# Ending the weight sums of a decoder trunk's down projection inside the gate/up groups, with a new table of rank shifts

## The chip, the cores and the metric

The kernel runs on one core of a Trainium2 chip. TensorE (PE, with its weight loads as PEld), VectorE (DVE), ScalarE (ACT), GpSimd (POOL) and SyncE (SP) each work through a queue of their own, in a fixed order, and meet at semaphores. The metric is the device time of one execution in microseconds (us): 2087.72 us as the median of 3 runs before the change (2087.07 to 2088.88).

## The reference

The reference is a decoder trunk of two layers over 1024 tokens of width 1024, in float32:

```python
for l in range(DEPTH):
    h = rmsnorm(x, attn_norm[l])
    proj = h @ w_in[l]                      # split into ten parts for four token mixers
    ...                                     # latent attention, gated convolution, pooling, window attention
    x = x + mixed @ w_o[l]
    h2 = rmsnorm(x, ffn_norm[l])
    gate, up = jnp.split(h2 @ w_gate_up[l], 2, axis=-1)
    x = x + (jax.nn.silu(gate) * up) @ w_down[l]
return rmsnorm(x, final_norm)
```

The feed-forward width is 2816. The change lies in the last two products, `w_gate_up` and `w_down`.

## The kernel before, in words

**Products.** Activations are held transposed, features on the 128 partitions, in two halves of 512 tokens. Each float32 operand is split into a high and a low part of type float32r: ACT casts the high part (L281) and DVE subtracts it for the low part (L282). Three matmuls of 128x512 (high-high, high-low, low-high, L270) then stand for one float32 product.

**Gate and up.** Both feed-forward products use a seven-product scheme on 2x2 blocks in place of eight products. The gate/up stage has 22 groups `f`; groups 1 to 21 go through one loop. A group forms seven sums of 12 matmuls, partly on top of one another in the same PSUM bank. Where a partial sum is needed twice, ACT copies it out of the bank (`snap`, L1180), and the next 12 matmuls on this bank wait for that copy. A group has three such copies: after the first sum, after the second sum on the same bank, and after the first sum on the other bank (`ps_mm`). The results of two groups are combined on DVE (`combos`) and written to HBM buffers `ad1` to `ad6` (L1329), and one half goes to `ad0` (L1461).

**Down.** The down stage has 28 units: seven products times four row blocks, 33 matmuls each. Each unit loads its weights (L1375), from `w_dn` or from the buffer `qd`, and its activations (L1392, L1395) from `ad`, and splits both on ACT and DVE.

**The sums of down weights.** `qd` holds four sums of blocks of `w_down`, as the scheme needs them. The generator `dn_sums` makes them in 22 pieces: load 512 KB (L155), four DVE adds (L159), store 512 KB to `qd` (L162). It yields three times a piece, so 66 steps lead to the last add, and a 67th issues the last store. Each loop group takes three steps (`next(sums, None)`), the last group none: 60 steps. The first five down units take three steps each, which is where the other pieces end.

**Buffers.** SBUF is 47 slots of 128x1024 float32, handed out by the program in its written order (`u17_7140` is the tile with number 7140, in slot 17). A load into a slot waits on SP until the last user of that slot is done. If that user is a store, SP waits until the store has landed, with all that is queued behind it.

**The order.** The order of the queues is not the order of the code. A planner (`order_engines`, `arrange`) takes all instructions with an estimated duration and a rank, which is the place in the program plus a shift, and lets each engine take the ready instruction with the lowest rank. The shifts stand in the table `MOVED`, as pairs of group and shift. The order that comes out is fixed for each engine: if on the chip an instruction is late, all behind it on that engine wait.

All loads and stores named here go through SP's queue.

Of the kernel before, what the change touches and what calls it, by code (L numbers as in the profile page):

```python
# [111 lines left out]
def trunk_kernel(ctx: ExitStack, tc: tile.TileContext, ins, out):  # L112
# [266 lines left out]
    for l in range(L):  # L379
# [84 lines left out]
        for t in range(2):  # L464
            f = tmp()
# [988 lines left out]
        for f in range(NPL, NFF):  # L1454
# [37 lines left out]
            if not end:  # L1492
                next(sums, None)
# [804 lines left out]
```

## Time and profile before

| What | Value |
|---|---|
| Median of 3 runs | 2087.72 us |
| Profiled execution, its own time | 2087.91 us |
| Its span, first to last instruction | 2086.1 us |
| PE busy | 2046.0 us, 98% of the span |
| DVE busy / ACT busy | 77% / 47% |
| Mean granted TensorE clock | 0.997 |
| Gate/up groups of the two layers | about 368 to 795 us and 1460 to 1822 us |
| Down stage, first units, of the two layers | from about 795 us and 1822 us |

The profiled execution took 1.8 us more than its span. PE counts as busy from a matmul's start to its modelled end, and matmuls overlap, so idle time of PE between matmuls is read from the rows of PE in order of time: a number in brackets at the end of a row is how long PE stood idle before it, and on what it waited. The chain of waits follows the work that ended last, back from the last instruction.

### The profile page before, as it was taken

What the parts mean: (1) busy time and instruction counts of PE and PEld (TensorE: products, weight loads), DVE (VectorE), ACT (ScalarE), POOL (GpSimd) and SP (SyncE); (2) the same over time, 40 slices, a digit from 0 to 9 for tenths busy, and PEclk for the clock granted to TensorE, in tenths of its full rate; (3) what the DMA queues carried; (4) which work ended last, traced back from release to release, by engine and by line L of the source; (5) the groups of instructions that cost most, each with busy time, mean ns of one, the idle gap of its engine ahead of it and who ended that gap; (6) DMA issues with size and microseconds to landing.
All of it is one profiled execution on the core that took longest, in us unless ns stands there. A gap on an engine that the chain in (4) does not pass through costs nothing.

```text
span 2086.1 us, 26084 instructions
## 1 busy us (share of the span) xinstructions
PE 2046.0 (98%) x9394; PEld 1666.1 (80%) x9394; DVE 1600.1 (77%) x2859; ACT 983.9 (47%) x1726; POOL 7.0 (0%) x37
## 2 busy tenths in 40 slices
PE   8999999999999999999999999999999999999997
PEld 6887887778878887788888877877878878877787
DVE  7789987997867877655656898989878787785465
ACT  6447666753333334444532576757333333354342
POOL 0000000000000000000000000000000000000000
PEclk9999999999999999999999999999999999999999
DMA  4110222345435438766411103142554444397562
GB/s 169 43 62 21 83 82 99 111 162 182 162 131 179 161 125 276 265 214 207 137 46 44 46 19 98 59 151 77 182 177 144 159 172 141 121 345 243 170 212 82
DMA packets 148817, 289.74 MB, mean 139 GB/s; under 512 B 12608, under 2 KB 72000, under 8 KB 148688
## 3 DMA queue, kind: packets, MB, share of 16 engines
q1 hardware_dynamic: 148656, 288.03, 40.7%
q8 instruction: 74, 1.21, 0.2%
q14 instruction: 55, 0.45, 0.1%
q0 software_dynamic: 32, 0.04, 0.0%
HBM read 204.66 MB, written 83.36 MB: 138 GB/s over the span
## 4 chain that ended last, share of the span: by engine, by line
PE 82%; DVE 8%; DMA 6%; ACT 2%; issue 2%; SPq 0%; DVEq 0%; ACTq 0%
PE ps_mm L270 33%; PE ps_s L270 23%; PE ps_t L270 9%; PE ps_pv L270 7%; PE ps_pv L966 2%; DVE u L282 2%; PE ps_t L954 1%; DMA u<-ad 1%; DMA u<-in_w_dn 1%; DMA ad<-u 1%; PE ps_t L328 1%; DVE u L285 1%; ACT u L281 1%; PE ps_s L900 1%; PE ps_s L901 1%
## 5 line engine op out<-in xcount | busy, mean ns | idle before, releaser
L270 PE MATMUL ps_mm<-u,u 128*128 128x512 f32 (+1 forms) x3376 | 880.8, 392 | 13.7 <-ACT u L284 7.0
L270 PEld LDWEIGHTS ps_mm<-u,u 128*128 128x128 f32 x3376 | 620.7, 189 | 149.0 <-issue 8.6
L270 PE MATMUL ps_s<-u,u 128*128 128x512 f32 x2666 | 685.1, 392 | 11.1 <-ACT tn L1180 7.1
L270 PEld LDWEIGHTS ps_s<-u,u 128*128 128x128 f32 x2666 | 497.0, 188 | 127.3 <-ACT tn L1180 13.9
L281 ACT CAST u<-u 128x1024 fp32r<-128x1024 f32 (+2 forms) x376 | 329.7, 897 | 492.2 <-PE ps_mm L270 111.5
L282 DVE TENSOR_TENSOR u<-u,u 128x1024 fp32r<-128x1024 f32 (+2 forms) x376 | 380.0, 1031 | 147.6 <-ACT u L281 122.3
L270 PE MATMUL ps_t<-u,u 128*128 128x512 f32 (+1 forms) x1122 | 294.0, 379 | 0.0
L270 PEld LDWEIGHTS ps_t<-u,u 128*128 128x128 f32 x1122 | 205.3, 188 | 41.4 <-ACT u L281 1.2
L270 PE MATMUL ps_pv<-u,u 128*128 128x512 f32 x744 | 203.3, 392 | 3.4 <-ACT u L281 1.7
L270 PEld LDWEIGHTS ps_pv<-u,u 128*128 128x128 f32 x744 | 138.3, 188 | 36.5 <-ACT u L281 3.3
L1314 ACT ACTIVATE tp<-tp 128x512 f32<-128x512 f32 x88 | 55.5, 632 | 98.3 <-DVE tp L340 98.2
L281 ACT CAST u<-ps_t 128x512 fp32r<-128x512 f32 (+3 forms) x128 | 60.1, 501 | 58.9 <-PE ps_t L954 33.2
L284 ACT ACTIVATE u<-u,par 128x512 fp32r<-128x512 f32 x100 | 69.4, 717 | 33.2 <-DVE u L1103 12.3
L282 DVE TENSOR_TENSOR u<-ps_t,u 128x512 fp32r<-128x512 f32 (+3 forms) x128 | 71.1, 576 | 13.1 <-ACT u L281 12.6
L1180 ACT COPY tn<-ps_s 128x512 f32<-128x512 f32 x64 | 37.3, 583 | 87.1 <-PE ps_s L270 87.0
L159 DVE TENSOR_TENSOR u<-u 128x256 f32<-128x256 f32 x176 | 73.9, 421 | 4.6 <-DMA u<-in_w_dn 3.0
L285 DVE SCALAR_TENSOR_TENSOR u<-u,par,u 128x512 fp32r<-128x512 f32 x100 | 72.6, 747 | 3.3 <-ACT u L284 3.2
L316 ACT ACTIVATE tn<-u 128x512 f32<-128x512 f32 (+1 forms) x93 | 52.3, 590 | 44.6 <-DVE u L1565 36.3
L214 DVE TENSOR_TENSOR u<-u,u 128x1024 fp32r<-128x1024 f32 (+1 forms) x46 | 51.8, 1128 | 25.8 <-ACT u L213 17.5
L1315 DVE TENSOR_TENSOR tp<-tp,u 128x512 f32<-128x512 f32 x88 | 60.3, 687 | 14.6 <-ACT tp L1314 14.4
L1512 DVE TENSOR_TENSOR tp<-ps_mm,tn 128x512 f32<-128x512 f32 x42 | 28.9, 689 | 49.7 <-PE ps_mm L270 49.5
L213 ACT CAST u<-u 128x1024 fp32r<-128x1024 f32 (+1 forms) x46 | 44.7, 975 | 29.7 <-DMA u<-in_w_in 11.8
(189 smaller groups left out, 2054.7 us busy)
## 6 DMA issues: line engine op xcount, KB each, us to landing
u<-in_w_gu SPq DMA_DIRECT2D x88, 512.0 KB, 4.0
ad<-u SPq DMA_DIRECT2D x154, 256.0 KB, 2.1
u<-ad SPq DMA_DIRECT2D x70, 512.0 KB, 5.1
u<-in_w_dn SPq DMA_DIRECT2D x68, 512.0 KB, 3.9
qd<-u SPq DMA_DIRECT2D x44, 512.0 KB, 3.2
u<-qd SPq DMA_DIRECT2D x32, 512.0 KB, 4.5
u<-in_w_in SPq DMA_DIRECT2D x30, 512.0 KB, 3.5
u<-in_xT SPq DMA_DIRECT2D x32, 256.0 KB, 4.5
```

The lines of the kernel that those rows point to most:

```text
L159: dve.tensor_tensor(out=o, in0=o, in1=u, op=ALU.add)
L213: act.copy(hi[:, :n], raw[:, :n])
L214: dve.tensor_tensor(out=lo[:, :n], in0=raw[:, :n], in1=rd(hi[:, :n]), op=ALU.subtract)
L270: pe.matmul(o, w, r, start=start and k == 0 and i == 0, stop=stop and k == n - 1 and i == 2, skip_group_check=again,)
L281: act.copy(hi, f)
L282: dve.tensor_tensor(out=lo, in0=f, in1=rd(hi), op=ALU.subtract)
L284: act.activation(hi, f, AF.Copy, scale=gain)
L285: dve.scalar_tensor_tensor(out=lo, in0=f, scalar=gain, in1=rd(hi), op0=ALU.mult, op1=ALU.subtract)
L316: act.activation(q, f, AF.Square)
L966: pe.matmul(py[:, c0:], v_of(j, h), R.ap(s)[:, c0:], start=j == 0 and n == 0, stop=j == nj - 1 and n == 1,)
L1314: last_silu = act.activation(g, g, AF.Silu)
L1315: dve.tensor_tensor(out=g, in0=g, in1=r, op=ALU.mult)
```

## The change

It has two parts. In the loop over the gate/up groups, the second of the three places that step `dn_sums` now takes one step in an even group and two in an odd one. Groups 1 to 20 then take 70 steps, which is over the 67 that all sums need, so that the calls in the down stage find nothing left. And the whole table `MOVED` is replaced: 1427 pairs in place of 1985, fitted with scattered DMA times.

```diff
             silu(gate, r2[0])
-            if not end:
+            for _ in range(0 if end else 1 + (f % 2)):
                 next(sums, None)
             onto(w.pa, blocks(w.sq, 0), hb[T3])
...
 MOVED = """
-1:-5.5 5:1 6:-403.5 7:-85.5 8:-2 10:5.5 11:9 12:-294.5 13:128 16:-110 17:21 19:24 20:4 22:23.5 23:45.5
...
+1:-15 5:-2.5 10:70.5 13:-497.5 16:67.5 20:-3.5 23:-3 26:-9 29:-220.5 54:-1 56:-98.5 80:-31 81:-340 82:5 83:-6
...
```

No matmul, cast, copy or DMA is added or removed. All engines' queues are put in another order. Three places show how.

**SP, where layer 0 goes from the gate/up groups to the down stage**, behind the stores to `ad` of groups 18 and 19. Before:

```order
L1375 DMA u17_7140<-in_w_dn 128x1024
L1392 DMA u31_7144<-ad0_87 128x1024
L1375 DMA u45_7141<-in_w_dn 128x384 x2
L1392 DMA u41_7165<-ad0_87 128x1024
L1392 DMA u1_7198<-ad0_87 128x1024
L162 DMA qd_94<-u15_7010 128x4x256
L155 DMA u31_7277<-in_w_dn 128x4x256
L1375 DMA u15_7463<-in_w_dn 128x1024
L1392 DMA u41_7330<-ad1_88 128x1024
L1392 DMA u46_7146<-ad0_87 128x1024
```

And now:

```order
L1329 DMA ad6_93<-u28_7020 128x512
L1375 DMA u41_7155<-in_w_dn 128x1024
L1375 DMA u36_7156<-in_w_dn 128x384
L1392 DMA u17_7159<-ad0_87 128x1024
L1375 DMA u36_7156<-in_w_dn 128x384
L1392 DMA u45_7182<-ad0_87 128x1024
L1375 DMA u12_7177<-in_w_dn 128x1024
L1392 DMA u39_7180<-ad0_87 128x1024
L1588 DMA u17_7294<-xr_86 128x512
L1392 DMA u33_7213<-ad0_87 128x1024
```

The store of a sums piece (L162) and the load of the next (L155) no longer stand among the first loads of the down stage. Before, the load into slot 15 (`u15_7463`) came two rows behind the store that reads the same slot (`u15_7010`); now no load there follows a sums store.

**ACT and PE in the same stretch**, in the last group (f = 21). On ACT, from the first copy out of the bank `ps_s` to the second. Before:

```order
L1180 COPY tn_7119<-ps_s_7105 128x512
L281 CAST u2_7201<-u41_7165 128x1024
L281 CAST u0_2157<-u28_6826 128x512
L281 CAST u5_7179<-u46_7146 128x1024
L281 CAST u7_7169<-u17_7140 128x1024
L1314 ACTIVATE tp_7087<-tp_7087 128x512
L281 CAST u0_2157<-u45_7141 128x384
L1180 COPY tn_7160<-ps_s_7105 128x512
```

And now:

```order
L1180 COPY tn_7134<-ps_s_7120 128x512
L281 CAST u1_7216<-u39_7180 128x1024
L281 CAST u6_7220<-u45_7182 128x1024
L281 CAST u23_7296<-u12_7177 128x1024
L281 CAST u0_2157<-u36_7156 128x384
L281 CAST u10_7285<-u33_7213 128x1024
L1180 COPY tn_7175<-ps_s_7120 128x512
```

On PE, from the end of the sum that the second copy takes to the next sum on its bank. Before:

```order
L270 MATMUL ps_s_7105<-u24_4207,u40_7032 128x512
L270 MATMUL ps_mm_7183<-u22_4053,u14_7068 128x512 x2
L270 MATMUL ps_mm_7183<-u22_4053,u12_7069 128x512
L270 MATMUL ps_mm_7183<-u42_4090,u14_7068 128x512
L270 MATMUL ps_s_7105<-u8_4057,u14_7068 128x512 x2
```

And now:

```order
L270 MATMUL ps_s_7120<-u24_4207,u32_7051 128x512
L270 MATMUL ps_mm_7198<-u22_4053,u46_7085 128x512 x2
L270 MATMUL ps_mm_7198<-u22_4053,u28_7086 128x512
L270 MATMUL ps_mm_7198<-u42_4090,u46_7085 128x512 x2
L270 MATMUL ps_mm_7198<-u42_4090,u28_7086 128x512
L270 MATMUL ps_mm_7198<-u26_4172,u46_7085 128x512 x2
L270 MATMUL ps_mm_7198<-u26_4172,u28_7086 128x512
L270 MATMUL ps_mm_7198<-u34_4210,u46_7085 128x512 x2
L270 MATMUL ps_mm_7198<-u34_4210,u28_7086 128x512
L270 MATMUL ps_s_7120<-u8_4057,u46_7085 128x512 x2
```

On ACT five casts of freshly loaded down tiles now stand between the two copies, where four stood (with one cast of a gate/up weight and one SiLU). On PE 12 matmuls on the other bank now stand between the sum that is copied and the next use of its bank, where 4 stood.

**SP in the gate/up groups of layer 0.** Before, at group 3:

```order
L1461 DMA ad0_87<-u25_3864 128x512
L1130 DMA u46_4372<-in_w_gu 128x1024
L1130 DMA u45_4373<-in_w_gu 128x1024
L155 DMA u27_4422<-in_w_dn 128x4x256
L1329 DMA ad3_90<-u15_4409 128x512
```

And now:

```order
L1130 DMA u45_4375<-in_w_gu 128x1024
L155 DMA u17_4351<-in_w_dn 128x4x256
L1461 DMA ad0_87<-u25_3864 128x512
L162 DMA qd_94<-u41_4273 128x4x256
L1130 DMA u41_4376<-in_w_gu 128x1024
L1329 DMA ad3_90<-u15_4412 128x512
```

A load of gate/up weights into slot 41 now stands right behind the sums store that reads slot 41. There are five such pairs in the gate/up groups of the two layers (two in layer 0, three in layer 1), and before there was none.

313 rows, old and new, of the table MOVED are left out of this document.

## The prediction

> **What bounds the kernel now.** I read the page first.
>
> ```profile
> span 2086.1 us, 26084 instructions
> PE 2046.0 (98%) x9394; PEld 1666.1 (80%) x9394; DVE 1600.1 (77%) x2859; ACT 983.9 (47%) x1726; POOL 7.0 (0%) x37
> ```
>
> PE stands idle for 2086.1 - 2046.0 = 40.1 us, and the change adds and removes no matmul. So the question is which part of these 40.1 us can go, or what can be added to them. Next, PE's busy time in stretches of 70 us (columns: stretch, its length, PE busy with its matmuls, granted clock, share of the DMA engines, GB/s):
>
> ```profile
> 0.00:70.00 70.00, 62.94 (x272) 1.00 0.37 134
> ...
> 770.00:840.00 70.00, 65.33 (x281) 0.98 0.73 253
> 840.00:910.00 70.00, 68.13 (x294) 0.98 0.74 248
> ...
> 1820.00:1890.00 70.00, 66.37 (x289) 1.00 0.90 318
> ...
> 2030.00:2100.00 70.00, 44.56 (x317) 0.94 0.20 68
> ```
>
> The start takes 70 - 62.94 = 7.1 us, the end 56.1 - 44.56 = 11.5 us. Between them 21.5 us are left. The stretches where gate/up turns into down (770 to 910 and 1820 to 1890) lose 4.7 + 1.9 + 3.6 = 10.2 us of that, and they are the ones in which the DMA engines are busiest. The waits there, from PE's rows in order of time (start, length, what, and in brackets the idle time before):
>
> ```profile
> 814.02 4.43 PE L270 MATMUL ps_s<-u,u 128*128 128x512 f32 x12 [4.67 <-ACT tn L1180]
> 881.72 8.66 PE L270 MATMUL ps_mm<-u,u 128*128 128x512 f32 x30 [1.87 <-DVE u L1565]
> 964.25 0.73 PE L270 MATMUL ps_pv<-u,u 128*128 128x512 f32 x2 [0.76 <-ACT u L281]
> ...
> 1836.42 1.20 PE L270 MATMUL ps_s<-u,u 128*128 128x512 f32 x4 [0.43 <-DVE te L1500]
> 1850.88 0.96 PE L270 MATMUL ps_s<-u,u 128*128 128x512 f32 x3 [1.63 <-ACT tn L1180]
> 1888.57 1.67 PE L270 MATMUL ps_mm<-u,u 128*128 128x512 f32 x6 [1.58 <-DVE u L282]
> 1954.90 0.50 PE L270 MATMUL ps_pv<-u,u 128*128 128x512 f32 x1 [0.95 <-ACT u L281]
> ```
>
> What made the ACT copy at 814 late is in the chain of waits, and in SP's own waits from 795 to 890 us (sum, times, longest):
>
> ```profile
> 795.04 6.43 DMA qd<-u
> ...
> 802.41 8.13 DMA u<-ad
> ...
> 811.52 1.04 ACT u L281
> ...
> SPq L1375 <- DMA qd<-u: 4.8, 2, 4.4
> ```
>
> The store of a sums piece, issued at 795.04, took 6.43 us to land. SP held the next weight load (L1375) for 4.4 us until then, because that load takes the store's slot. The activation loads behind it went out late and took 8.13 us. ACT's casts waited for them, and the copy (L1180) that PE needed stood behind the casts. Layer 1 has the same link in its chain:
>
> ```profile
> 1822.04 4.28 DMA u<-in_w_dn
> ...
> 1841.90 6.10 DMA u<-in_w_dn
> ...
> 1873.37 5.42 DMA qd<-u
> ...
> 1879.24 5.75 DMA u<-ad
> ```
>
> The sums load of 1822.04 leads by its adds to the wait at 1836.42, and the sums store of 1873.37 by a held load to the wait at 1888.57. The wait at 1850.88 follows the late down load of 1841.90, in which no sums piece stands.
>
> **An idle wait costs more than its length.** Granted clock and PE busy time around the waits:
>
> ```profile
> 810.26:813.67 3.41, 0.00 (x0) 1.00 0.95 365
> 878.52:881.94 3.42, 1.55 (x7) 1.00 0.30 84
> 1847.81:1851.22 3.41, 1.78 (x9) 1.00 0.97 343
> 813.68:817.08 3.40, 3.06 (x7) 0.50 0.27 102
> 881.94:885.35 3.41, 3.41 (x9) 0.50 0.92 289
> ```
>
> Behind the waits at 814.02 and 881.72 the clock was 0.50 for 3.41 us each, which loses 3.41 / 2 = 1.7 us of work. Behind the wait at 1850.88 it stayed at 1.00 (its row is the one with 1.78 us busy). [...]
>
> **The change part by part.** *Which pieces move.* 60 steps were taken in the groups and 67 are needed, so per layer two loads (L155), eight adds (L159) and three stores (L162) of 0.524 MB each move, 2.6 MB. Nothing is saved in total. Their cost where they go:
>
> ```profile
> 368.00:795.00 427.00, 425.54 (x1853) 344.11 (x1852) 352.47 (x548) 172.76 (x248) 0.00 (x0) 1.00 0.45 156
> 795.00:890.00 95.00, 88.45 (x375) 71.70 (x373) 59.27 (x77) 42.36 (x54) 0.00 (x0) 0.96 0.78 267
> L159 DVE TENSOR_TENSOR u<-u 128x256 f32<-128x256 f32 x176 | 73.9, 421 | 4.6 <-DMA u<-in_w_dn 3.0
> ```
>
> (Columns: PE, PEld, DVE, ACT, POOL busy, then clock, DMA share, GB/s.) In the groups DMA moves 427 us x 156 GB/s = 67 MB, so 2.6 MB are 4% more and the share goes from 0.45 to 0.47. The adds are 8 x 0.42 = 3.4 us of DVE, which has 427 - 352 = 75 us free there. PE covers both, and without that cover the adds would cost their 3.4 us a layer. In the stretch from 795 to 890 the same 2.6 MB are 10% of its 95 x 267 GB/s = 25.4 MB, that is 9.7 us of transfer.
>
> *Layer 0, the wait at 814.* Its price now is 4.67 + 1.7 = 6.4 us. The sums store goes, and with it SP's 4.4 us. PE now has 12 matmuls in place of 4 between the sum that is copied and the next use of its bank. One matmul takes 0.227 us:
>
> ```profile
> 1995.64 37.49 PE ps_s L270 x165
> ```
>
> So the cover grows by 8 x 0.227 = 1.8 us. Against it ACT has one more down cast between the two copies, 1.04 us (the gate/up cast and the SiLU that no longer stand there I don't count). 4.67 - 4.4 - 1.8 + 1.04 is about -0.5: the wait goes, by half a microsecond, which is too thin to trust. I leave 0.5 us of it and take a gain of 5.9 us. Bounds: 0 (other loads are just as late) and 6.4.
>
> *Layer 0, the wait at 881.72.* Price 1.87 + 1.7 = 3.6 us. It ends a long run of late loads, in which the moved bytes are one part and the slots of `ad` stores another. I take half, 1.8 us. Bounds 0 and 3.6.
>
> *Layer 1, the waits at 1836, 1850 and 1888.* Price 0.43 + 1.63 + 1.58 = 3.6 us, with sums in the chain of the first and the third. I take half, 1.8 us. Bounds 0 and 3.6.
>
> *964 and 1954.* Sums are long over there (their last store is at 1873.37). Gain 0.
>
> *The gate/up groups.* The new table touches every wait in them:
>
> ```profile
> 421.62 1.20 PE L270 MATMUL ps_s<-u,u 128*128 128x512 f32 x4 [0.78 <-ACT tn L1180]
> 454.13 0.96 PE L270 MATMUL ps_pv<-u,u 128*128 128x512 f32 x3 [0.41 <-DVE u L282]
> ...
> 1453.65 0.96 PE L270 MATMUL ps_pv<-u,u 128*128 128x512 f32 x3 [1.24 <-DVE tn L333]
> 1562.01 0.73 PE L270 MATMUL ps_s<-u,u 128*128 128x512 f32 x2 [2.54 <-ACT u L281]
> 1715.23 0.96 PE L270 MATMUL ps_s<-u,u 128*128 128x512 f32 x3 [0.99 <-DVE u L282]
> ```
>
> Together 6.0 us. The order alone doesn't say which go and which come, since these follow single late landings. I take 0, with -6.0 (all go) and +6.0 (as many again) as bounds. The same holds for the attention stages, where single waits of about 1 us stand; I add nothing for them, nor for start and end.
>
> **Sum.** 5.9 + 1.8 + 1.8 = 9.5 us. The profiled execution took 2087.9 us (span 2086.1 and 1.8 around it): 2087.9 - 9.5 = 2078.4. The median of the runs is 0.2 us under that execution, so **2078.2 us**.
>
> **The rivals.**
>
> *A. The wait stays, only its cause changes.* In the new ACT order the second copy stands behind five casts of fresh down tiles. The loads of these follow six stores to `ad` in SP's queue, and if they land as late as the 8.13 us above without any sums store, the copy is as late as before. For it: the DMA share of 0.73 to 0.90 falls only by a tenth. Against it: SP's longest hold on a sums store, 4.4 us, is almost the whole wait. Then only some of layer 1 is gained, about 1 us: 2086.7 us.
>
> *B. SP stands still in the groups instead.* In the new order five loads of gate/up weights stand right behind the sums store of their own slot. Each holds SP until the store has landed, 4.4 us at the one measured, and holds the other gate/up loads and `ad` stores behind it. At 814 such a hold cost 6.4 us. If three of the five cost that, it is 19.2 - 9.5 = 9.7 us slower, **2097.6 us**; with two it is 12.8 - 9.5 = 3.3 us, which can't be told from no change, so it decides from the third on. Against it: of ACT's waits from 380 to 780 us only one kind ends with a DMA, and it is not a gate/up load, so these loads have room before their use:
>
> ```profile
> ACT u L281 <- DMA ad<-u: 3.4, 2, 3.2
> ```
>
> *C. Everything named goes.* If the groups' waits vanish with those of the transitions, it is 6.4 + 3.6 + 3.6 + 6.0 = 19.6 us, and 2068.1 us. For it: the groups' waits come from landings that vary. Against it: no row shows that the new order has more room at those places.
>
> **How the numbers follow.** About 0.2% (4.2 us) is what a measurement of this kernel can tell from no change. The forecast, a gain of 4.2 to about 16 us, gets 0.62. A gets 0.18, all within 0.2%. B gets 0.14, all slower, with what else a new order of every queue can spoil. C gets 0.06, faster. So faster 0.68, same 0.18, slower 0.14. The forecast's own range is 2071 to 2083.5. The range for 8 in 10 takes in A and reaches to C at 2068 below. Above it reaches to 2091, the two-hold case of B, and leaves the rest of B out.
>
> **What would show it.** Right, if PE's waits near 795 to 890 and 1822 to 1892 us sum to under 4 us with no stretch at clock 0.50, SP has no wait of L1375 on a `qd` store there, and the DMA share there is lower by 0.05 to 0.1. The step on the wait at 814 is wrong if PE still waits there for an L1180 copy of more than 1 us. The zero for the groups is wrong if their waits sum to over 8 or under 4 us. The forecast as a whole fails if new waits in groups or attention outweigh the 9.5 us, which B would show as SP waits of L1130 on `qd` stores.

## The result, and the profile after

The kernel after takes **2061.18 us** (median of 4 runs), and the kernel before took 2088.30 us (median of 4). The ratio is 0.9872, with a 95% interval of 0.9855 to 0.9889. It is faster by 27.1 us. Medians in this document are over all runs and ratios over the fast ones; one run each of `e10_oldloop_scatter` (3199 us) and `e11_best` (5301 us) was slow, which moves their medians by under 0.5 us. The forecast was 2078.2 us, a gain of 9.5, with a range down to 2068: right in sign, and wrong in size by a factor of almost three.

The page of the kernel after:

```profile
span 2059.1 us, 26108 instructions
PE 2035.2 (99%) x9394; PEld 1671.3 (81%) x9394; DVE 1607.4 (78%) x2859; ACT 988.1 (48%) x1726; POOL 6.7 (0%) x37
```

The span fell by 27.0 us. PE's idle time fell from 40.1 to 2059.1 - 2035.2 = 23.9 us, which is 16.2 us. The other 10.8 us came out of PE's *busy* time, 2046.0 to 2035.2, with the same 9394 matmuls. The same windows of the kernel after that were shown of before (PE busy, then the other engines, clock, DMA share, GB/s):

```profile
0.00:70.00 70.00, 62.95 (x278) 50.95 (x279) 53.41 (x104) 43.96 (x81) 0.86 (x5) 1.00 0.38 134
368.00:795.00 427.00, 425.08 (x1861) 347.71 (x1860) 356.94 (x556) 174.59 (x248) 0.00 (x0) 1.00 0.49 165
795.00:890.00 95.00, 95.00 (x421) 78.64 (x419) 65.24 (x79) 48.95 (x62) 0.00 (x0) 1.00 0.77 265
1820.00:1890.00 70.00, 70.00 (x311) 57.95 (x310) 46.67 (x57) 35.80 (x45) 0.00 (x0) 1.00 0.76 262
```

Behind the gate/up groups PE is now busy without a break, at full clock: 421 matmuls in the 95 us that held 375 before. Most transfers did not get shorter; only the activation loads (`u<-ad`) gained 0.3 us in the median. The rows of DMA issues (KB each, median us from issue to landing), first before, then after:

```profile
u<-in_w_gu SPq DMA_DIRECT2D x88, 512.0 KB, 4.0
ad<-u SPq DMA_DIRECT2D x154, 256.0 KB, 2.1
u<-ad SPq DMA_DIRECT2D x70, 512.0 KB, 5.1
qd<-u SPq DMA_DIRECT2D x44, 512.0 KB, 3.2
```

```profile
u<-in_w_gu SPq DMA_DIRECT2D x88, 512.0 KB, 4.2
ad<-u SPq DMA_DIRECT2D x154, 256.0 KB, 2.3
u<-ad SPq DMA_DIRECT2D x70, 512.0 KB, 4.8
qd<-u SPq DMA_DIRECT2D x44, 512.0 KB, 3.6
```

Nor does ACT wait less for them. Its waits on activation loads (sum, times, longest), before and after:

```profile
ACT u L281 <- DMA u<-ad: 93.3, 46, 7.7
```

```profile
ACT u L281 <- DMA u<-ad: 88.0, 47, 8.8
```

So landings are on the whole as late as before, and ACT stands about as long. What changed is that PE no longer stands with it.

**A better measure than idle time.** A row of one matmul and a row of many show why idle time told too little. From PE's rows of the kernel after, and its chain of waits:

```profile
773.04 0.39 PE L270 MATMUL ps_s<-u,u 128*128 128x512 f32 x1
```

```profile
860.70 14.96 PE ps_mm L270 x66
```

One matmul counts as busy for 0.39 us (its end is modelled), but the next can start after 14.96 / 66 = 0.227 us. A matmul that starts up to 0.16 us late leaves no idle time at all, and every visible wait costs 0.16 us more than its bracket says. From here on I therefore count the **loss**: the time from one matmul's start to the next, less the start-to-start time that such a matmul takes undisturbed (0.227 us at 512 columns; the medians of the trace for the narrower ones), summed over a stage. The stages are cut at the same matmul of PE's queue in every kernel. In the kernel before, the groups of layer 0 are counted from behind the wait at 421.62 us, and the stages behind the groups reach past the waits at 964.25 and 1954.90 us. Us, one profiled execution each:

```
                            up to     groups   behind   up to     groups   behind   end   sum
                            groups 0  layer 0  them     groups 1  layer 1  them
before                       11.7      3.9     11.4       8.2      9.1      6.3     1.7   52.3
after                        11.1      1.0     -0.4       7.3      3.8      0.0     2.4   25.1
e1_table_only                10.8      6.5      0.8       8.3     11.4      1.2     2.3   41.4
e2_sums_only                 11.5     12.7      8.0       7.2     16.4      7.8     1.7   65.3
e3_before_drop               11.1      4.3      2.3       7.4      8.8      3.0     1.7   38.6
e4_after_traffic             10.5      1.1      4.9       8.0      3.3      6.7     2.3   37.0
e7_after_nohold              10.7      1.4      4.9       7.4      3.2      1.1     2.3   31.1
e5_before_load               11.1     15.0      7.3      11.3     18.7      8.3     1.7   73.3
e6_after_load                15.0     22.1     -0.4       7.2     21.2      1.0     2.3   68.4
e8_fit_fixed                 12.1      8.4      8.9       8.4     11.3      6.8     1.7   57.7
e12_fit_fixed2                9.8      7.1      9.4       8.2     11.5      8.7     1.7   56.6
e9_fit_scatter               11.8      3.2      6.0       6.5      3.7      0.1     2.5   33.8
e13_fit_scatter2             13.2      3.7      0.1       7.9      5.6      0.2     1.2   32.0
e10_oldloop_scatter          15.8      7.6      2.7       7.2      7.9      1.0     0.9   43.0
e14_oldloop_scatter2         13.6      5.2      3.0       7.5      7.5      1.8     7.5   46.2
e11_best                     10.0      2.2      0.1       6.8      3.4      1.8     1.8   26.2
e15_best2                    10.6      1.7      0.0       7.0      3.3      0.3     2.0   25.0
```

Small differences between columns and sums are rounding. The first two rows divide the gain of 27: 18.1 us behind the groups (11.4 + 6.3 to -0.4), 8.2 us in the groups (13.0 to 4.8), and under 1 us elsewhere. In the four stages of groups and down products together the loss was 30.7 us, of which 17.1 showed as idle time. It is now 4.4.

### The profile page after: what moved, and what is told of

Same layout as the page of the kernel before. It is cut to its first block, busy times and chain, and to the rows that moved or that the text cites. A ratio compares the mean times of both kernels' runs of the same rounds, so it can differ in the third digit from the quotient of the medians.

```text
span 2059.1 us, 26108 instructions
## 1 busy us (share of the span) xinstructions
PE 2035.2 (99%) x9394; PEld 1671.3 (81%) x9394; DVE 1607.4 (78%) x2859; ACT 988.1 (48%) x1726; POOL 6.7 (0%) x37
## 4 chain that ended last, share of the span: by engine, by line
PE 94%; DVE 3%; ACT 1%; DMA 1%; issue 1%; SPq 0%; DVEq 0%; ACTq 0%
PE ps_mm L270 36%; PE ps_s L270 28%; PE ps_t L270 11%; PE ps_pv L270 8%; PE ps_pv L966 2%; PE ps_t L954 1%; PE ps_t L328 1%; PE ps_s L900 1%; PE ps_s L901 1%; PE ps_s L902 1%; PE ps_pv L566 1%; PE ps_s L505 1%; PE ps_mm L765 1%; PE ps_t L554 1%; DVE u L282 1%
## 5 line engine op out<-in xcount | busy, mean ns | idle before, releaser
L270 PE MATMUL ps_mm<-u,u 128*128 128x512 f32 (+1 forms) x3376 | 864.4, 390 | 9.3 <-ACT u L284 7.1
L281 ACT CAST u<-u 128x1024 fp32r<-128x1024 f32 (+2 forms) x376 | 329.2, 897 | 482.7 <-PE ps_mm L270 126.1
L282 DVE TENSOR_TENSOR u<-u,u 128x1024 fp32r<-128x1024 f32 (+2 forms) x376 | 381.9, 1032 | 168.8 <-ACT u L281 144.3
L270 PE MATMUL ps_t<-u,u 128*128 128x512 f32 (+1 forms) x1122 | 282.9, 379 | 0.5 <-DVE u L1565 0.5
L270 PE MATMUL ps_pv<-u,u 128*128 128x512 f32 x744 | 197.7, 390 | 0.0
L281 ACT CAST u<-ps_t 128x512 fp32r<-128x512 f32 (+3 forms) x128 | 60.8, 501 | 51.4 <-PE ps_t L554 23.9
L282 DVE TENSOR_TENSOR u<-ps_t,u 128x512 fp32r<-128x512 f32 (+3 forms) x128 | 71.5, 576 | 13.0 <-ACT u L281 12.7
L1180 ACT COPY tn<-ps_s 128x512 f32<-128x512 f32 x64 | 37.4, 584 | 91.3 <-PE ps_s L270 90.9
L1315 DVE TENSOR_TENSOR tp<-tp,u 128x512 f32<-128x512 f32 x88 | 60.4, 689 | 11.7 <-ACT tp L1314 11.5
L340 DVE TENSOR_TENSOR tp<-tp,u 128x512 f32<-128x512 f32 x84 | 57.7, 689 | 0.6
```

The source lines that it names most:

```text
L270: pe.matmul(o, w, r, start=start and k == 0 and i == 0, stop=stop and k == n - 1 and i == 2, skip_group_check=again,)
L281: act.copy(hi, f)
L282: dve.tensor_tensor(out=lo, in0=f, in1=rd(hi), op=ALU.subtract)
L340: dve.tensor_tensor(out=o, in0=a, in1=b, op=ALU.mult)
L1315: dve.tensor_tensor(out=g, in0=g, in1=r, op=ALU.mult)
```

## The experiments

Two theories stood at the start. **Sums:** the late pieces of the sums delay the first loads of the down stage, and taking them away is the gain. **Table:** the new order leaves more time between a landing and the matmul that needs it, and that is the gain.

### Each part alone

`e1_table_only`: the loop of before, with the order of the new table carried over step by step.

```diff
-    for g in groups(steps):
-        for v in g:
-            v.shift = moved.get(g[0].rank, 0.0)
+    for v in steps:
+        v.shift = moved.get(float(v.rank), 0.0)
...
-1:-5.5 5:1 6:-403.5 7:-85.5 8:-2 10:5.5 11:9 12:-294.5 13:128 16:-110 17:21 19:24 20:4 22:23.5 23:45.5
+1:-15 5:-2.5 10:70.5 13:-497.5 16:67.5 20:-3.5 23:-3 26:-9 29:-220.5 30:-220.5 31:-220.5 32:-220.5
...
```

> The old loop (60 steps of the sums in the groups, the rest in the down stage) with the new table: each instruction keeps the rank and the shift that it has in the changed kernel, and the last pieces of the sums keep their late place in the program. The sums theory (the late pieces delay the loads where gate/up turns into down): the waits there come back for the most part, 2061.2 + 8 to 14, so 2069 to 2075 us, with PE waits of over 4 us in all between 795 and 890 us or 1822 and 1892 us. The table theory (the order gives late landings room, and the sums' place hardly matters): 2060 to 2064 us, no stretch at half clock there.

Measured: 2076.24 us, ratio 0.9934 (0.9919 to 0.9949).

`e2_sums_only`: the loop of after, with the old table's order carried over in the same way.

```diff
-            if not end:
+            for _ in range(0 if end else 1 + (f % 2)):
                 next(sums, None)
```

> The new loop (all sums end in the groups) with the old table: each instruction that is not of the sums keeps the rank and the shift that it had before. The sums theory: the 8 to 14 us of the two transitions are gained and the groups' waits stay, 2088.3 - 8 to 14, so 2074 to 2080 us. The table theory: nothing is gained, and the old table may fit the new ranks a little worse, 2084 to 2096 us.

Measured: 2102.86 us, ratio 1.0062 (1.0047 to 1.0077), which is slower. Both runs lie above the ranges of both theories, and neither part gives 27 us. The table alone cleared the stages behind the groups (17.7 to 2.0 us of loss) although the late pieces still stood there, but the groups got worse (13.0 to 17.9). PE's waits of `e1_table_only` in the groups:

```profile
456.00 2.60 PE L270 MATMUL ps_pv<-u,u 128*128 128x512 f32 x10 [1.63 <-DVE u L282]
723.72 0.97 PE L270 MATMUL ps_s<-u,u 128*128 128x512 f32 x3 [2.92 <-ACT u L281]
...
1482.58 0.73 PE L270 MATMUL ps_t<-u,u 128*128 128x512 f32 x2 [1.94 <-ACT u L281]
```

A carried-over order fits neither program well, so these two runs say that the parts do not simply add up, and little more.

### What the late pieces cost

`e3_before_drop`: the kernel before in its own order, without the late pieces.

```diff
     def dn_sums(l):
...
-            sp.dma_start(v, ins["w_dn"][l, :, :, cols].rearrange("b p n -> p b n"))
+            if not (leave and in_down[0]):
+                sp.dma_start(v, ins["w_dn"][l, :, :, cols].rearrange("b p n -> p b n"))
...
-            sp.dma_start(qd[:, :, cols].rearrange("b p n -> p b n"), v)
+            if not (leave and in_down[0]):
+                sp.dma_start(qd[:, :, cols].rearrange("b p n -> p b n"), v)
...
+        if leave:
+            tail_cols = slice(19 * HT // 2, NK // 2 * NG * P)
+            sp.dma_start(qd[:, :, tail_cols], ins["w_dn"][l, :, :, tail_cols])
```

> The kernel before with its own order, out of which only the late pieces of the sums are taken: per layer two loads, eight adds and three stores in the down stage are left out, and their part of the sums buffer is filled early with unsummed weights, so the output is another. Every other instruction stands where it stood. The sums theory: the waits at 814, 1836 and 1888 us go and half of the one at 881, so 2088.3 less 8 to 12, 2076 to 2080 us. The table theory: the order is as tight as it was and other late landings take their place, 2083 to 2088 us.

Measured: 2075.31 us, ratio 0.9930 (0.9916 to 0.9945). `e4_after_traffic` is the other way round: the kernel after, with dead transfers where the pieces stood in SP's queue.

```diff
+        for k in range(5):
+            back = junk[4 * l] if k == 1 else ins["w_dn"][l, 0, :, 1024 * k : 1024 * (k + 1)]
+            sp.dma_start(junk[4 * l + (k if k < 2 else 2 + k % 2)], back)
         nxt = []
         for r in first.popleft():
```

> The changed kernel with the late pieces' transfers put back as dead copies inside HBM: per layer five copies of 512 KB in SP's queue at the places, counted from the first down load, where the kernel before had its two sums loads and three sums stores; the second reads what the first wrote, so that SP is held until the first has landed, as it was at 795 us. The sums theory: PE waits come back, 5 to 12 us, 2066 to 2073 us, the first near 800 to 815 us. The table theory: the new order has the room, 2061 to 2063 us.

Measured: 2074.32 us, ratio 0.9927 (0.9911 to 0.9944), 13.1 us above the kernel after. Both runs agree that the late pieces cost some 13 us behind the groups in these two orders, and nothing in the groups; `e1_table_only` carried the same pieces with a loss of 2.0 us there, so this price belongs to the order as much as to the pieces. In `e3_before_drop` the loss behind them falls from 17.7 to 5.3 us and the groups stay at 13.1. Five waits of PE are left there:

```profile
873.98 13.20 PE L275 MATMUL ps_mm<-u,u 128*128 128x512 f32 x57 [0.91 <-DVE u L1574]
954.88 0.74 PE L275 MATMUL ps_pv<-u,u 128*128 128x512 f32 x2 [0.69 <-ACT u L286]
...
1826.04 3.92 PE L275 MATMUL ps_s<-u,u 128*128 128x512 f32 x16 [0.62 <-DVE te L1509]
1839.45 3.06 PE L275 MATMUL ps_s<-u,u 128*128 128x512 f32 x12 [0.64 <-ACT tn L1189]
1941.17 0.50 PE L275 MATMUL ps_pv<-u,u 128*128 128x512 f32 x1 [0.48 <-ACT u L286]
```

`e7_after_nohold` takes SP's standing still out of `e4_after_traffic`:

```diff
-            back = junk[4 * l] if k == 1 else ins["w_dn"][l, 0, :, 1024 * k : 1024 * (k + 1)]
-            sp.dma_start(junk[4 * l + (k if k < 2 else 2 + k % 2)], back)
+            sp.dma_start(junk[5 * l + k], ins["w_dn"][l, 0, :, 1024 * k : 1024 * (k + 1)])
```

> The kernel after with five dead transfers of 512 KB per layer (HBM to HBM) at the places in SP's queue where the late loads and stores of the sums stood before, as in the run e4_after_traffic (2074.3 us), but now none of them waits for another: in that run the second one read what the first wrote, so SP stood still until the first had landed. If it was SP's standing still that cost 13 us there, this one takes 2061 to 2065 us, and the stages behind the gate/up groups (795 to 890 us and 1820 to 1892 us) keep PE at 100% busy. If it was the traffic itself, it takes 2071 to 2076 us and PE waits there again for 5 us and 7 us over its pitch.

Measured: 2067.51 us, ratio 0.9881 (0.9865 to 0.9896), between the two. PE's waits behind the groups, first with SP held and then without:

```profile
826.37 8.68 PE L272 MATMUL ps_s<-u,u 128*128 128x512 f32 x30 [3.18 <-DVE u L1310]
1827.59 5.49 PE L272 MATMUL ps_s<-u,u 128*128 128x512 f32 x12 [3.80 <-ACT tn L1182]
```

```profile
827.21 8.70 PE L272 MATMUL ps_s<-u,u 128*128 128x512 f32 x30 [3.40 <-DVE u L1310]
1824.81 3.04 PE L272 MATMUL ps_s<-u,u 128*128 128x512 f32 x12 [0.94 <-ACT tn L1182]
```

In layer 1 the held queue made the wait (3.80 against 0.94 us). In layer 0 the traffic alone made it (3.18 and 3.40). By the medians it is about half and half: 6.8 us for the hold and 6.3 for the traffic.

### More traffic for both kernels

If the new order simply has more room for late landings, it should bear extra traffic better. Both kernels got a dead copy of 512 KB behind each gate/up load.

```diff
                 for n in range(2):
                     sp.dma_start(F.ap2(self.raw[n]), ins["w_gu"][l, f, n])
+                    sp.dma_start(junk[(2 * f + n) % 8], ins["w_gu"][l, f, n])
```

> The kernel before, in its own order, with one dead transfer added behind each of the 88 loads of gate/up weights in SP's queue: the same 512 KB again, from the weights in HBM to a scratch tensor in HBM that nobody reads. Nothing waits for it; it only makes the landings around it later. It is one half of a pair with the next run. Theory 'room': the new table left more time between a landing and its first use in the gate/up groups, and that is where the 8 us come from that the groups gained (loss over the matmuls' own pitch in the groups: 13.0 us before, 4.8 after). Then the kernel before, which has no such room, loses 20 to 50 us. Theory 'any fit' (the groups gained because the table was fitted to the program that runs, and landings have nothing to do with it): it loses as much as the kernel after does in the next run, within 5 us.

> The kernel after with the same 88 dead transfers of 512 KB at the same places. 'Room': 3 to 12 us over the kernel after (2064 to 2073), less than half of what the kernel before loses by them. 'Any fit': the two lose alike, within 5 us.

Measured: 2111.33 us for before (ratio 1.0092, 1.0074 to 1.0109), which is 21 us up, and 2102.76 us for after (ratio 1.0051, 1.0035 to 1.0066; ten runs from 2095.5 to 2107.2), which is 41.6 us over the 2061.18 of the first runs. Both theories missed: the kernel after bears this traffic *worse*. SP's waits on a sums store, in the kernel after and in `e6_after_load`:

```profile
SPq L1130 <- DMA qd<-u: 16.8, 5, 4.0
```

```profile
SPq L1132 <- DMA qd<-u: 26.8, 6, 7.4
```

These are gate/up loads into the slot of a sums store (L1132 is L1130 with two lines added above it), the place of rival B. The kernel before and `e5_before_load` have no such wait. The chain of waits of `e6_after_load` around one of its long waits:

```profile
1711.24 0.35 SPq L1132
...
1712.23 7.56 DMA qd<-u
...
1724.32 1.76 PE ps_pv L272 x5
```

PE had waited 2.42 us there. Other waits of that run end on chains with a sums load of 7.91 us (layer 0) and with `ad` stores of 6.2 to 6.9 us. So the new loop has a coupling that the old one lacks. No run with the old loop has an SP wait of a gate/up load on a sums store, and every run with the new loop has four or more. How long such a hold may be before PE waits is not fixed: in `e11_best` below the longest is 6.0 us, and that kernel is about as fast as the kernel after. That the coupling accounts for all of the 20 us between the two kernels is not shown.

### How the table is fitted

The change says that the new table was fitted with scattered DMA times. Two fits of our own were made for this, from the same old table and with the same kind of random moves of groups of steps, in the kernel's own planner. One keeps a move if the plan with fixed DMA times ends earlier, until it ends no later than the plan of the kernel after. The other draws twelve sets of random extra landing times, keeps each engine's order fixed, and keeps a move if the mean end over them is earlier. Only the table differs, with the line that reads it step by step. How the old table itself was fitted is not on record.

```diff
-    for g in groups(steps):
-        for v in g:
-            v.shift = moved.get(g[0].rank, 0.0)
+    for v in steps:
+        v.shift = moved.get(float(v.rank), 0.0)
...
-1:-15 5:-2.5 10:70.5 13:-497.5 16:67.5 20:-3.5 23:-3 26:-9 29:-220.5 54:-1 56:-98.5 80:-31 81:-340 82:5 83:-6
+0:255 1:430.5 2:-493 4:408.5 5:-5 6:-15 8:-1 10:392 12:0.5 13:165.5 14:30.5 15:-535 16:-286 17:-1 18:-4
...
```

> The loop of the kernel after (sums end within the groups) with a table of rank shifts of our own: from the old table, steps were moved at random in the kernel's own planner, every DMA taking its fixed time, and a move was kept if the plan ended earlier, until the plan ended no later than that of the kernel after. Nothing else differs from the kernel after. Theory 'scatter': what PE waits for on the chip is landings that come later than the plan has them, so a table that was fitted with fixed times leaves PE waiting in the gate/up groups however well its plan ends: 2078 to 2105 us, with the groups' loss over the matmuls' own pitch at 12 to 30 us for both layers (kernel after: 4.8). Theory 'fit': a table need only be fitted to the program that it runs in; then this one is as good as the new table: 2060 to 2068 us, groups' loss 4 to 8 us.

> The same loop, the same start (the old table) and the same kind of moves, but each order is judged by its mean end over twelve draws in which every transfer of SP's queue lands later by a random time (exponential, 0.7 us in the mean). It differs from the run before only in that. 'Scatter': 2050 to 2064 us, groups' loss under 5 us. 'Fit': as the run before, within 4 us.

> The loop of the kernel before (the last pieces of the sums behind the groups, among the transfers of the down products) with a table fitted in the same scattered way from the old one. 'Scatter' alone, with no part for the place of the sums: 2052 to 2066 us, within 5 us of the run before, and no wait of PE over 1.5 us behind the groups. 'Sums' (the late pieces cost some 13 us behind the groups whatever the table, as e3 and e4 read): 2066 to 2078 us, with a loss of 5 to 13 us left in the two stages behind the groups.

A second draw of each:

> As e8_fit_fixed (loop of the kernel after, table fitted with fixed DMA times from the old one), with another series of random moves. One fit is one draw; this one says how far draws lie apart. If the way of fitting decides: 2085 to 2100 us, within 8 us of e8_fit_fixed (2093.2) and over 10 us above both scattered fits of this loop. If e8 was an unlucky draw: 2060 to 2080 us.

> As e9_fit_scatter (loop of the kernel after, scattered fit from the old table; 2069.6 us), with other moves and other draws. If the way of fitting decides: 2060 to 2074 us.

> As e10_oldloop_scatter (loop of the kernel before, scattered fit from the old table; 2078.2 us), with other moves and other draws. If the place of the sums is worth something of its own beside the fit (8.6 us between e9 and e10): 2070 to 2082 us, above both scattered fits of the new loop, and above the run e13 by 4 us or more. If not, and e9 against e10 was the luck of two draws: within 4 us of e13, or under it.

Measured (us, ratio to the kernel before, 95% interval):

| | table fitted to fixed DMA times | table fitted to scattered DMA times |
|---|---|---|
| late pieces (old loop) | not run; the kernel before, with the old table, took 2090.3 and 2090.7 beside these runs | e10 2078.21, 0.9941 (0.9919 to 0.9963); e14 2078.95, 0.9941 (0.9925 to 0.9957) |
| sums end in the groups (new loop) | e8 2093.22, 1.0013 (1.0003 to 1.0022); e12 2091.89, 1.0006 (0.9991 to 1.0021) | e9 2069.61, 0.9906 (0.9884 to 0.9928); e13 2069.21, 0.9891 (0.9876 to 0.9906) |

Two draws of one kind lie within 1.4 us, so the kind decides, not the luck of a draw. With a table fitted to fixed times, moving the sums gains **nothing**, although by the planner's own fixed times such an order ends no later than that of the kernel after. On the old loop a table fitted with scatter is 12 us faster than the old table, and on the new loop it is 23 us faster than one fitted to fixed times. (The 2069.6 us of e9 still lie above the 2050 to 2064 that were expected of it.) With it, the place of the sums is worth about 9 us (2078.6 to 2069.4), although the loss table puts 6 us of the distance of e14 at its end, so 7 in the stages concerned: 19.2 and 17.5 on the old loop, 13.0 and 9.6 on the new. Where the last 8 us to the kernel after come from is not shown: how its table was fitted, beyond the words of the change, is not on record.

The same runs say what the late pieces are worth. `e8_fit_fixed` issues its last sums store inside the groups (772 us in layer 0, 1803 us in layer 1), and still loses 8.9 + 6.8 us behind the groups, against 11.4 + 6.3 in the kernel before; `e10_oldloop_scatter` has the late pieces and loses 2.7 + 1.0. PE's two longest waits of `e8_fit_fixed` there:

```profile
847.68 1.22 PE L270 MATMUL ps_pv<-u,u 128*128 128x512 f32 x2 [3.81 <-ACT u L281]
...
1882.13 0.73 PE L270 MATMUL ps_mm<-u,u 128*128 128x512 f32 x2 [1.97 <-ACT u L281]
```

So taking the pieces away helps an order that was made around them (`e3_before_drop`), but an order without room waits there for other casts.

**What stays open.** The draws add 0.7 us to each transfer in the mean, beside making them uneven. The planner's own times lie below the medians on the chip: by its formula in the kernel (`wire` and `v.end` in `arrange`) a load of 512 KB with nothing ahead of it takes 1.4 + 1.31 + 0.47 + 0.28 = 3.46 us and a store 2.66, where the kernel before measured medians of 4.0 and 3.2. A fit with fixed but longer times was not run, so whether the unevenness or the longer time makes the better table is not shown. Nor is it on record how many moves each fit tried.

The same windows in layer 1's groups (PE busy, count), for e8, e9 and e10 in this order:

```profile
1440.00:1800.00 360.00, 353.91 (x1537) 284.71 (x1536) 292.00 (x457) 134.76 (x187) 0.00 (x0) 1.00 0.49 166
```

```profile
1440.00:1800.00 360.00, 359.41 (x1571) 291.81 (x1570) 293.62 (x461) 131.90 (x184) 0.00 (x0) 1.00 0.50 168
```

```profile
1440.00:1800.00 360.00, 356.86 (x1553) 287.77 (x1552) 286.34 (x448) 132.55 (x185) 0.00 (x0) 1.00 0.47 160
```

Between the first two the matmuls of the program are the same and the traffic is nearly so (166 against 168 GB/s), and PE idles 6.1 us with the one table and 0.6 with the other.

**What such a table may do.** For each operand that L281 (ACT) or L282 (DVE) writes for PE between 368 and 900 and between 1420 and 1900 us, I took the time from the end of the write to the first matmul that reads it, matched by the order of the queues (some 410 to 440 operands a kernel, without the eight or so whose match gave a time below zero). How many of them were ready less than 0.5 us ahead:

```
before                69      median lead 10.4 us
e8  / e12 (fixed)     65 / 65             9.2 / 9.2
e10 / e14 (old loop)  63 / 53            10.5 / 9.9
e9  / e13 (new loop)  46 / 54            10.1 / 10.1
e1                    25                 14.2
e11 / e15             25 / 26            12.8 / 12.5
after                 17                 14.1
```

One of the 69 stands in the profile of before. ACT's row at the fourth wait that the prediction listed for the groups (1562.01, 2.54 us):

```profile
1560.91 2.52 ACT L281 CAST u<-u 128x1024 fp32r<-128x1024 f32 x3 [3.23 <-DMA ad<-u]
```

ACT waited 3.23 us for a landing, and the first of its three casts ended 0.05 us before PE's matmul at 1562.01. PE stood idle from 1559.47 us, so through the last 1.44 us of ACT's wait and the cast behind it. The reading that fits is this: a plan with fixed times sees no difference between a lead of 0.05 us and one of 10 us as long as the landing is on time, so the fixed fits leave about a sixth of all operands just in time (65 each), and a landing that is late by some tenths can then delay PE. This is argued, not shown, and the lead is not the whole story: `e10_oldloop_scatter` has 63 such operands, hardly fewer than the fixed fits, and is 12 us faster than the kernel before, while `e1_table_only` has leads like the best kernels, and loses 13 us more in the groups than the kernel after (17.9 against 4.8, by single waits of up to 2.92 us).

### Whether more is to be had

`e11_best` and `e15_best2` fit the new table further with scatter.

> The loop of the kernel after, with the new table fitted further in the same scattered way (mean 0.7 us). 'Scatter': 2050 to 2060 us, since some 5 us of the groups' loss and the attention stages' waits are left to gain. 'Fit': 2060 to 2063 us, as the kernel after.

> The table of e11_best (2062.7 us) fitted further on the loop of the kernel after, with a wider scatter (1.0 us in the mean, sixteen draws). If margin ahead of TensorE still buys time: 2054 to 2060 us. If what is left of the loss (25 us: start, end, the attention stages' pauses) has nothing to do with landings: 2060 to 2064 us, as e11_best and the kernel after.

Measured: 2062.66 us (ratio 0.9868, 0.9847 to 0.9890) and 2061.26 us (0.9864, 0.9843 to 0.9885), level with the kernel after. Of the 25 us of loss that are left, 20.8 stand at the start, in the attention stages and at the end, and these fits hardly moved it. The 2050 to 2060 us that the scatter theory expected of them were not reached.

## Why the prediction was right in sign and wrong in size

**The base of the sum.** "The question is which part of these 40.1 us can go" is the step that failed first. Idle time fell by 16.2 us, and 10.8 us came from time in which PE counted as busy. In the stages of groups and down products 13.6 of the 30.7 us of loss were of that kind, nearly all of it in three parts: 97 starts late by 0.02 to 0.17 us (7.4 us; now 36, 3.0 us), 0.16 us beside each visible wait, and the two stretches of half clock. The prediction priced only the last of these.

**The wait at 814.** Forecast gain 5.9 of 6.4 us, and it went altogether. The reading of its cause holds in part: with the late pieces gone and nothing else changed (`e3_before_drop`) no wait is left there, but `e7_after_nohold` shows that, in the new order, traffic at that place makes a wait of 3.40 us without any hold of SP. The prediction gave the hold almost the whole of it.

**The waits at 881.72, 1836, 1850 and 1888.** "I take half" was wrong: they went whole, 7.2 us for 3.6 forecast. Of the 7.2, `e3_before_drop` leaves waits of 0.91, 0.62 and 0.64 us and no half clock behind them, so the late pieces alone were worth some 5 us and the new order the rest. **964 and 1954**, "gain 0", went too (0.76 + 0.95 us). From 760 to 1000 us PE has no wait left. `e3_before_drop` still has both (0.69 and 0.48 us), so their going is the table's for the most part.

**The groups, "I take 0".** The second failing step. Their loss fell by 8.2 us, of which some 4.5 us was visible as idle time (5.2 to 0.7 in the table's stages). From 368 to 770 and from 1420 to 1822 us, which is a little wider, PE's waits are now 1.4 and 0.5 us in layer 0 and 0.5, 0.4 and 0.2 us in layer 1, together 3.0 us where the prediction counted 6.0. That is under the bound of 4 that was named for calling the zero wrong. The prediction held that the order alone doesn't say which waits go, "since these follow single late landings". That may be so of each one, but it was wrong of their sum. The change names scattered DMA times, and no term of the prediction asks what such a fit does: on the new loop it was worth 23 us between `e8_fit_fixed` and `e9_fit_scatter`, of which 12.8 us in the groups.

**The rivals.** A fell: no wait of L1180 is left at 814, SP has no wait of L1375 on a `qd` store there, and PE did not wait behind the five casts ahead of the copy. B was right about the mechanism and wrong about the price: SP stands still behind a sums store at five places, for 16.8 us in all, but the groups lose 4.8 us where they lost 13.0, so no loss like the 6.4 us a hold that B feared came of it. Under the traffic of `e6_after_load` such places hold for up to 7.4 us, and at least one reaches PE. C, "everything named goes", with a chance of 0.06, came nearest, with 19.6 us and 2068.1: its transition waits went whole (13.6 us), the groups' waits by half (3.0 of 6.0), and the two zeros (964, 1954) gave 1.7 more, 18.3 us together. The rest of the 27 us is loss that no wait shows. Against C stood "no row shows that the new order has more room at those places"; the result shows that it has.

**The signs that were named.** No half clock and no wait of PE from 795 to 890 and 1820 to 1890: as forecast. The DMA share there: 0.90 to 0.76 in layer 1 as forecast, but 0.78 to 0.77 in layer 0, probably because the faster kernel brings other transfers into the window. The groups' share rose from 0.45 to 0.49, where 0.47 was forecast.

## What to carry to other kernels

Read the loss of a saturated engine from start to start against its undisturbed pitch, not from its idle time: here 13.6 of 30.7 us did not show as idle. The orders fitted to the planner's fixed transfer times planned as well as the kernel after and ran 23 us slower than those fitted to scattered, on average longer ones; fit the order against landings as the chip has them, and refit it whenever the program's steps move, since moving the sums without such a fit gained nothing here. Before giving a change of order the price "zero, can't be told", ask what the new order was fitted against, and look at how many operands are ready less than half a microsecond ahead of their use; that count goes with the loss here, but it is no price.

## What the hardware showed

**Half clock behind a wait.** In the kernel before, the granted clock changed at 813.67, 817.09, 881.94 and 885.35 us, which are whole multiples of 3.41 us apart. On that grid, from 8 to 2040 us, five of its 595 windows hold under 2.0 us of PE's busy time. The two with 0.00 and 1.55 us, which the prediction shows, were followed by a window at half clock. The other three were not (window, PE busy, ..., clock, DMA share, GB/s; the second row of each is the next window):

```profile
1557.79:1561.20 3.41, 1.68 (x8) 1.06 (x6) 2.45 (x3) 0.29 (x1) 0.00 (x0) 1.00 0.97 374
1561.21:1564.61 3.40, 2.60 (x11) 2.17 (x12) 2.10 (x3) 2.86 (x4) 0.00 (x0) 1.00 0.09 34
1847.92:1851.33 3.41, 1.78 (x8) 1.16 (x8) 2.81 (x5) 2.60 (x7) 0.00 (x0) 1.00 0.95 336
1851.34:1854.74 3.40, 3.40 (x17) 2.79 (x16) 3.40 (x7) 1.99 (x3) 0.00 (x0) 1.00 0.59 176
1885.46:1888.87 3.41, 1.83 (x8) 1.24 (x7) 2.72 (x3) 3.41 (x5) 0.00 (x0) 1.00 0.61 184
1888.88:1892.28 3.40, 3.40 (x16) 2.76 (x15) 2.37 (x3) 1.38 (x2) 0.00 (x0) 1.00 0.89 344
```

The kernel after has no such window under 2.33 us, and no half clock, in the same stretch. Two windows of other runs lie close together: 1.59 us in `e5_before_load`, followed by half clock, and 1.60 us in `e10_oldloop_scatter`, followed by full clock:

```profile
819.35:822.76 3.41, 1.59 (x8) 1.02 (x7) 1.55 (x3) 3.41 (x6) 0.00 (x0) 1.00 0.93 333
822.77:826.17 3.40, 3.40 (x9) 2.62 (x9) 3.40 (x5) 2.18 (x3) 0.00 (x0) 0.50 0.33 124
```

```profile
461.24:464.65 3.41, 1.60 (x7) 1.34 (x8) 1.32 (x2) 1.04 (x1) 0.00 (x0) 1.00 0.37 131
464.66:468.06 3.40, 3.40 (x17) 2.80 (x16) 3.40 (x6) 0.63 (x1) 0.00 (x0) 1.00 0.00 2
```

The two windows at half clock of the kernel before, with 3.06 and 3.41 us busy, were followed by full clock. In `e6_after_load` one with 2.27 of 3.39 us busy was followed by another at half clock:

```profile
533.97:537.38 3.41, 1.56 (x6) 0.66 (x4) 3.38 (x6) 2.98 (x4) 0.00 (x0) 1.00 0.42 122
537.39:540.78 3.39, 2.27 (x5) 1.84 (x6) 3.39 (x6) 0.00 (x0) 0.00 (x0) 0.50 0.99 322
540.80:544.20 3.40, 3.40 (x9) 2.67 (x8) 1.93 (x5) 0.00 (x0) 0.00 (x0) 0.50 1.02 421
```

So the price of a wait could not be read off its length here: the 1.87 us before 881.72 in the kernel before, all in one window, cost another 1.7 us, and the 2.54 us before 1562.01, of which 1.73 lay in one window and 0.80 in the next, no half clock. That this split made the difference is the likely reading; no run varied it, and these rows do not say what decides between half and full clock.

**A held queue is not a price.** SP stood still for 16.8 us behind sums stores in the kernel after, and its groups still lost only 4.8 us in all. In `e4_after_traffic` holds on one transfer in each layer, 10.6 us together, cost 6.8 us. That the room of the loads behind the hold decides is the likely reading; no run varied it alone.
